# DeltaNet in the program's own order: all five engines instead of the builder's scheduler

## The chip, the core and the metric

The kernel runs on one core of one Trainium2 chip. The metric is the device time of one execution in microseconds (us). Five engines work beside each other, each through its own queue of instructions: PE (TensorE, matrix products; PEld is its loading of weights), ACT (ScalarE, functions and scaled copies), DVE (VectorE, elementwise work), POOL (GpSimd) and SP (SyncE, which here issues transfers). An instruction starts when those before it on its engine have started and what it reads and writes is free; an instruction that waits holds up everything behind it in its queue. So the order in which an engine's instructions stand matters as much as their durations.

## The reference, cut to what matters

A trunk of two layers over 256 latent tokens and 256 context tokens, 1024 wide, in fp32. Each layer is FFN, token mixer, FFN. The mixer of layer 0 is a recurrent block; the mixer of layer 1 is a gated DeltaNet in both directions, with 8 heads of 128 x 128 and chunks of 64 tokens. What it computes per head and direction, for each chunk:

```
kb    = k * beta
a_mat = strict_lower((kb @ k.T) * decay) + I
u, w  = solve(a_mat, [v * beta, kb * exp(g_cum)])     # unit lower triangular
qk    = (q @ k.T) * decay
# scan over the chunks, first the context's, then the latents'
v_new = u - w @ s
o     = q_dec @ s + qk @ v_new
s     = s * g_tot + k_dec.T @ v_new
```

q, k, v and z come from one projection `h @ w_in` (q, k, v through a convolution of four taps and SiLU; q and k are normalized). The output is `rms_norm(o) * silu(z)`, projected with `w_out` and added to the latents. Only the latents go on from there to the last FFN.

## The kernel before, in words

**Stages.** Both FFNs of layer 0, the recurrent block and the first FFN of layer 1 come first (to about 1314 us of the span), then DeltaNet (1314 to about 1626, its output projection running on from there), then the last FFN, on latents alone.

**Products.** An fp32 product is three fp32r products (L301, L302, L303: high by high, high by low, low by high). A weight tile is loaded raw, then split by an ACT cast (L165) and a DVE subtraction (L166) into a pair, in a ring of eight pairs and three raw tiles; some tiles were split earlier and are loaded as pairs by POOL's queue. `WS.step()` issues one such split.

**Projections of DeltaNet.** 32 tiles in the order eight k, eight q, then v and z mixed (`vvvvzzvzzvvzzvzz`). The first four k tiles are done together with the norm. The other 28 go through one loop: k and v tiles in two halves (context and latents), q and z in one; a half is 24 products of 256 columns. Through each half four calls of `tick(n)` are made, and these spread the other engines' work between the products:

```python
def tick(n):
    WS.step()
    if n >= PACE["decay_from"]:
        run(dec, PACE["decay_steps"])
    pipe.tick(PACE["steps"])
    if n >= PACE["keys_from"]:
        run(later, 1)
```

`pipe` holds the heads that have been projected: `conv` (ACT copy L787, three DVE operations L791), SiLU, and what q, k and v need after it (L1145, L1150; L1168 multiplies q's products into the decay). `later` is `keys()`, one of whose steps is taken per tick from tile 9 on (`keys_from` = 9). It makes the decay matrices of the eight heads (`k_rest`, L1086 to L1121, with Relu L1088 and Exp L1089 on ACT; four ticks a head), then the norms, and then

```python
for _ in solve():
    yield from pause(PACE["solve"])
```

with `PACE["solve"]` = 4. `solve` inverts the triangular blocks of all heads, chunks and directions at once: two DVE transposes, 31 elimination steps of one product (L1225, into `tm`) and one subtraction (L1228, into `Bc`), then four transposes (L1231, L1232). `merge` (L1247 to L1282) puts the 32 x 32 blocks together to 64 x 64 with small PE products. What `keys()` has not done at the end of the loop is done by `run(later)` right behind it (L1347), ahead of `pipe.drain()` and the scan.

**Scan.** 8 steps (four of the context, four of the latents) for each of 8 heads, which go in pairs. A pair passes through stages, and `advance` moves every live pair by one, the newest first. For latents: PE's p1 (L1386, state by k and q); DVE's L1394 (the right side r) and ACT's L1399 (a scaled copy of the same p1, four to a pair); PE's p2 (L1406) from r; ACT's L1409 and L1412 (two scaled copies of p2); PE's L1417 and DVE's L1424 (the new state); PE's p4 (L1430) and DVE's L1431 (added to the output).

**Readout.** `out_norm` of a head is called in `advance` when its last step is done: two squares with a sum on ACT (L1449); with the second head of a pair, a chain of small DVE operations (L1457 to L1461 and an inverse root by three Newton steps in integers and fp32, L315 to L324) and the scaling of two heads (L1463). When all pairs are through, `out_head` (PE transposes L1468, DVE L1471 and L1472, ACT cast L165, DVE L166) is called for heads 0 to 3, then for each further head ahead of the output projection's k-th batch of products. Its first residual is L750.

**What sets the order.** By default the builder's scheduler orders each engine's instructions: it simulates when each becomes ready and takes the earliest, the program's order being the priority. Where the code stands in `with eng("...")` (L151, `tc.manual_schedule`), the engines named (P: PE, A: ACT, D: DVE, G: POOL, S: SP) keep the program's order. Before, DeltaNet stands in no such block; the last FFN stands in `eng("PADGS")`.

Of the kernel before, what the change touches and what calls it, by code (L numbers as in the profile page):

```python
# [94 lines left out]
def trunk(ctx, tc, io):  # L95
# [9 lines left out]
    def nm(p):  # L105
        cnt[0] += 1
        return f"{p}{cnt[0]}"
# [4 lines left out]
    @contextmanager  # L112
    def phase(ns, nraw=0, nw=0, off=0):

        with tc.tile_pool(name=nm("ph"), bufs=1, reuse_waits="tile") as p:
            old = dict(scope)
            scope.update(s=p, ns=ns)
            if off:
                p.tile([128, off // 4], F32, name="pad1")
            if nw:  # L120
                slot("first")
            if off:
                p.tile([128, 64 - off // 4], F32, name="pad2")
            if nw:
                ring_l = Ring(p, "l", nraw, nw)
                ring_l.pair()
                ring_l.raw()
                WS.cycle("glglglglglglgg", "gggl" if nraw == 1 else "gglgl", ring_l)
            else:
                WS.cycle("g", "g", None)  # L130
            yield
            scope.clear()
            scope.update(old)
# [17 lines left out]
    def eng(E):  # L151
        return tc.manual_schedule(engines={dict(P=ET.PE, A=ET.Activation, D=ET.DVE, G=ET.Pool, S=ET.SP)[c] for c in E})
# [15 lines left out]
    class Ring:  # L168
# [8 lines left out]
        def pair(self):  # L177
            t = self.pool.tile([128, 2, 512], F32R, name=nm("wp"), tag="wp" + self.name, bufs=self.nw)
            return HL(t[:, 0], t[:, 1], t)
# [1444 lines left out]
    def front():  # L1624
        later = [t + {"q": 0, "v": 16, "z": 24}[x] for x, t in DN_ORDER[8:]]
        later = [("dn_in", t) for t in (*range(12, 16), *later)]
        outs = [("dn_out", d) for d in range(KD)]
        kept = later[PACE["kept_from"]:] + outs[:PACE["kept_out"]]
        WS.keep.extend(kept)
        norms = [Norm(0, 0), Norm(0, 1), Norm(0, 2), Norm(1, 0), Norm(1, 1, perm=True)]  # L1630
        parts = [Ffn(0, 0), Lru(), Ffn(0, 1), Ffn(1, 0)]
        WS.plan.extend((io["dn_in"][t], 1024, "g") for t in range(8, 12))
        WS.plan.append((io["dn_ab"], 256, "g"))
        assert not WS.keep
        WS.plan.extend((t, 1024, "p") if t in kept else (io[t[0]][t[1:]], 1024, "g") for t in later + outs)
        parts.append(Ffn(1, 1, (1,)))
        for i, p in enumerate(parts[:4]):
            with eng("PS" if i in (1, 2) else "PADGS"):
                if i == 0:
                    start(norms[0], p, norms[1], parts[1].prepare)  # L1640
                else:
                    p.run(norms[i], norms[i + 1], ahead=4)
        return norms[4], parts[4]

    with eng("PS"), phase(44, 2, 6):
        norm, f = front()
    adap.release()
    next_norm = Norm(1, 2, short=True)
    with tc.tile_pool(name="dns", bufs=1, reuse_waits="tile") as dns, phase(7):
        WS.ahead(4)  # L1650
        hpool = tc.alloc_tile_pool(name="hp", bufs=1, reuse_waits="tile")
        H = [hpool.tile([128, KD, 2, 256], F32R, name=nm("H"), tag=f"H{v}", bufs=1) for v in V2]
        ks = iter(range(KD))

        def pair(_):
            k = next(ks)
            return HL(*(Parts(H[0][:, k, i], H[1][:, k, i]) for i in range(2)))
        norm.pair = pair

        pools = [hpool, None, xctx]  # L1660

        def done(i):
            pools[i].release()
            if i == 2:
                pools[1] = tc.alloc_tile_pool(name="solve", bufs=1, side="right", reuse_waits="tile")

        deltanet(norm, next_norm, dns, hpool, pools, done)
    last = Norm(0, 0, short=True)
    with eng("PADGS"), phase(44, 2, 6, 192):
        WS.ahead(4)  # L1670
# [98 lines left out]
```

## Time and profile before

| | |
|---|---|
| median of 3 runs | 1841.48 us (1838.37 to 1845.29) |
| the profiled execution | 1840.58 us |
| its span | 1838.8 us |
| PE busy | 1767.9 us (96%) |
| PEld busy | 1534.4 us (83%) |
| DVE busy | 1311.3 us (71%) |
| ACT busy | 807.0 us (44%) |
| POOL busy | 105.6 us (6%) |
| chain that ended last, by engine | PE 79%, DVE 10%, ACT 5%, issue 4%, DMA 2% |

The shares are averages over stages with different limits. The stretches of DeltaNet must be looked at one by one: a table of windows gives each engine's busy time in a stretch, and a timeline of one engine gives its instructions in the order in which they ran, each with the wait before it and what ended this wait.

### The profile page before, as it was taken

To read this page: it belongs to the slowest core of one execution; us is meant where nothing else is said; L and a number is where in the kernel's file an instruction comes from. 1 tells how busy PE (TensorE), PEld (TensorE's weight loads), DVE (VectorE), ACT (ScalarE), POOL (GpSimd) and SP (SyncE) were. 2 spreads that over 40 slices of the span, in tenths; PEclk is the share of its full clock that TensorE was granted. 3 is DMA by queue.
4 is the path that set the end of the run, shared out by engine and by line. 5 is a ranking of instruction groups with operands and counts; after the bars stand their busy time and mean duration, and the time that the engine had idled before them with its cause. 6 is when DMAs were issued, how large, how long until landed. Compare 5 with 4: busy or idle time off the path is not lost.

```text
span 1838.8 us, 28624 instructions
## 1 busy us (share of the span) xinstructions
PE 1767.9 (96%) x10806; PEld 1534.4 (83%) x10806; DVE 1311.3 (71%) x2694; ACT 807.0 (44%) x1661; POOL 105.6 (6%) x146
## 2 busy tenths in 40 slices
PE   4999999999899999999999999999999989889997
PEld 3788888888778888888898888888997988689997
DVE  7877866787878767766657655555689978776565
ACT  5532222246884433233334331332478434655454
POOL 4100000000000000000000000000006330100000
PEclk9999999999999999999999999999999989989999
DMA  9354645452133666466633675654335550025653
GB/s 348 113 185 158 220 160 171 160 200 89 46 115 126 215 214 223 178 228 207 215 113 126 218 247 198 218 199 136 105 99 166 171 175 1 1 104 188 202 184 116
DMA packets 98059, 300.59 MB, mean 163 GB/s; under 512 B 10881, under 2 KB 20353, under 8 KB 97793
## 3 DMA queue, kind: packets, MB, share of 16 engines
q1 hardware_dynamic: 92160, 277.79, 44.7%
q0 software_dynamic: 5760, 20.97, 3.7%
q8 instruction: 85, 1.39, 0.3%
q14 instruction: 54, 0.43, 0.1%
HBM read 276.70 MB, written 22.02 MB: 162 GB/s over the span
## 4 chain that ended last, share of the span: by engine, by line
PE 79%; DVE 10%; ACT 5%; issue 4%; DMA 2%; POOL 0%; SPq 0%; POOLq 0%; ACTq 0%; DVEq 0%
PE gu L302 14%; PE gu L301 14%; PE gu L303 14%; PE fo L303 4%; PE fo L302 4%; PE fo L301 4%; PE tl L301 4%; PE tl L302 4%; PE tl L303 4%; DVE u L791 2%; PE p L1386 1%; PE gu L546 1%; PE gu L542 1%; PE gu L543 1%; PE p L1417 1%
## 5 line engine op out<-in xcount | busy, mean ns | idle before, releaser
L165 ACT CAST wp<-wr 128x512 fp32r<-128x512 f32 (+1 forms) x689 | 382.7, 607 | 279.8 <-DMA wr<-in_ffn_out_dram 68.1
L166 DVE TENSOR_TENSOR wp<-wr,wp 128x512 fp32r<-128x512 f32 (+1 forms) x689 | 433.5, 676 | 98.9 <-ACT wp L165 95.3
L302 PE MATMUL gu<-hl,wp 128*128 128x512 f32 (+1 forms) x1312 | 477.0, 364 | 8.0 <-DVE hl L505 8.0
L301 PE MATMUL gu<-hh,wp 128*128 128x512 f32 (+1 forms) x1312 | 476.9, 363 | 0.9 <-ACT hh L503 0.8
L303 PE MATMUL gu<-hh,wp 128*128 128x512 f32 (+1 forms) x1312 | 476.2, 363 | 0.0
L407 DVE SCALAR_TENSOR_TENSOR junk<-ar,cb 128x1024 bf16<-128x1024 f32 x224 | 273.8, 1223 | 22.6 <-DMA ar<-in_w_adaT_dram 18.8
L302 PEld LDWEIGHTS gu<-hl,wp 128*128 128x128 f32 x1312 | 247.3, 189 | 49.0 <-DVE hl L505 10.3
L301 PEld LDWEIGHTS gu<-hh,wp 128*128 128x128 f32 x1312 | 247.4, 189 | 41.2 <-ACT hh L503 1.6
L303 PEld LDWEIGHTS gu<-hh,wp 128*128 128x128 f32 x1312 | 247.5, 189 | 38.8
L657 ACT ACTIVATE sg<-gu 128x512 f32<-128x512 f32 (+1 forms) x88 | 47.9, 544 | 362.0 <-PE gu L303 352.3
L659 DVE TENSOR_TENSOR hf<-sg,gu 128x512 f32<-128x512 f32 (+1 forms) x88 | 54.5, 620 | 177.2 <-PE gu L303 130.3
L301 PE MATMUL tl<-hidh,wp 128*128 128x256 f32 (+1 forms) x418 | 139.1, 333 | 0.0
L302 PE MATMUL tl<-hidl,wp 128*128 128x256 f32 (+1 forms) x418 | 138.6, 332 | 0.0
L303 PE MATMUL tl<-hidh,wp 128*128 128x256 f32 (+1 forms) x418 | 138.6, 332 | 0.0
L301 PE MATMUL fo<-hidh,wp 128*128 128x512 f32 (+1 forms) x352 | 127.0, 361 | 0.0
L303 PE MATMUL fo<-hidh,wp 128*128 128x512 f32 (+1 forms) x352 | 127.0, 361 | 0.0
L302 PE MATMUL fo<-hidl,wp 128*128 128x512 f32 (+1 forms) x352 | 127.0, 361 | 0.0
L301 PE MATMUL f<-H,wp 128*128 128x256 f32 x320 | 93.2, 291 | 0.0
L303 PE MATMUL f<-H,wp 128*128 128x256 f32 x320 | 91.4, 286 | 1.0 <-DVE wp L166 1.0
L302 PE MATMUL f<-H,wp 128*128 128x256 f32 x320 | 91.2, 285 | 0.0
L301 PEld LDWEIGHTS tl<-hidh,wp 128*128 128x128 f32 x418 | 79.0, 189 | 7.9
L302 PEld LDWEIGHTS tl<-hidl,wp 128*128 128x128 f32 x418 | 79.0, 189 | 7.8
(322 smaller groups left out, 2794.7 us busy)
## 6 DMA issues: line engine op xcount, KB each, us to landing
wr<-in_ffn_in_dram SPq DMA_DIRECT2D x172, 512.0 KB, 4.7
ar<-in_w_adaT_dram SPq DMA_DIRECT2D x128, 512.0 KB, 3.6
wr<-in_ffn_out_dram SPq DMA_DIRECT2D x64, 512.0 KB, 4.9
kp<-wp SPq DMA_DIRECT2D x80, 256.0 KB, 7.2
wp<-kp POOLq DMA_DIRECT2D x40, 512.0 KB, 5.0
wr<-in_dn_in_dram SPq DMA_DIRECT2D x32, 512.0 KB, 3.7
wr<-in_ffn_out_dram SPq DMA_DIRECT2D x64, 192.0 KB, 3.5
wr<-in_lru_in_dram SPq DMA_DIRECT2D x16, 512.0 KB, 3.9
```

Source lines behind the costliest of these rows:

```text
L165: ACT.copy(dst.hi, src)
L166: DVE.tensor_tensor(dst.lo, src, dst.hi.bitcast(F32), OP.subtract)
L301: PE.matmul(out, w.hi, x.hi, start=start, stop=False)
L302: PE.matmul(out, w.hi, x.lo, start=False, stop=False)
L303: PE.matmul(out, w.lo, x.hi, start=False, stop=stop)
L407: DVE.scalar_tensor_tensor(junk, raw, 1.0, cb[:, v], OP.mult, OP.mult, accum_out=m[:, t % 8, v:v + 1])
L542: PE.matmul(p[:, cols], w.hi, x.hi, start=(k == 0), stop=False)
L543: PE.matmul(p[:, cols], w.lo, x.hi, start=False, stop=False)
L546: PE.matmul(p[:, cols], w(k * 128).hi, x.lo, start=False, stop=(k == KD - 1))
L657: ACT.activation(sg[:, cols], P[0][:, cols], AF.Silu)
L659: DVE.tensor_tensor(hf[:, cols], sg[:, cols], P[1][:, cols], OP.mult)
L791: DVE.scalar_tensor_tensor(uv[:, :, a:b], pv[:, :, a + sh:b + sh], cw(j), uv[:, :, a:b], OP.mult, OP.add)
```

## The change

The call of `deltanet` is put into `eng("PADGS")`: in DeltaNet each of the five engines issues its instructions in the order in which the program calls them. No instruction of the program, no size and no buffer is changed.

```diff
-        deltanet(norm, next_norm, dns, hpool, pools, done)
+        with eng("PADGS"):
+            deltanet(norm, next_norm, dns, hpool, pools, done)
```

## Rows read from the trace of the kernel before

**Rows 1.** Windows by stage: us, busy of PE, PEld, DVE, ACT, POOL, PEclk, DMA share, GB/s

```profile
1384.00:1432.00 48.00, 42.52 (x399) 36.18 (x398) 46.48 (x116) 42.97 (x86) 33.38 (x47) 0.97 0.52 162
1432.00:1445.00 13.00, 13.00 (x153) 11.87 (x153) 12.05 (x30) 6.27 (x24) 5.20 (x9) 0.85 0.25 81
1445.00:1497.00 52.00, 51.60 (x451) 51.13 (x449) 50.50 (x86) 18.70 (x52) 16.80 (x27) 1.00 0.75 231
1497.00:1521.00 24.00, 16.98 (x559) 16.29 (x560) 11.72 (x18) 9.13 (x19) 7.28 (x11) 0.72 0.26 82
...
1548.00:1601.00 53.00, 50.55 (x341) 39.83 (x340) 41.46 (x141) 35.44 (x112) 5.44 (x12) 1.00 0.00 1
1601.00:1626.00 25.00, 20.70 (x137) 19.03 (x136) 21.06 (x106) 15.16 (x56) 1.83 (x4) 0.80 0.00 1
```

**Rows 2.** Windows, line L1225 alone: us, DVE busy, PEclk, DMA share, GB/s

```profile
1474.00:1498.00 24.00, 5.72 (x12) 1.00 0.79 240
```

**Rows 3.** Windows, line L1228 alone, same columns

```profile
1474.00:1498.00 24.00, 5.75 (x12) 1.00 0.79 240
```

**Rows 4.** Timeline of DVE, end of the solve: start, us, engine, line, operation

```profile
1489.53 2.23 DVE L1231 STREAM_TRANSPOSE A<-Bc 128x1024 f32<-128x1024 f32 x1
...
1495.62 1.95 DVE L1232 STREAM_TRANSPOSE Bc<-Bc 128x1024 f32<-128x1024 f32 x1
1497.40 2.27 DVE L791 SCALAR_TENSOR_TENSOR u<-f,cst,u 128x510 f32<-128x510 f32 x3
```

**Rows 5.** Timeline of PE, the last product of the projections

```profile
1496.15 0.28 PE L303 MATMUL f<-H,wp 128*128 128x256 f32 x1
```

**Rows 6.** Timeline of DVE, readout: in brackets, idle before and its releaser

```profile
1604.62 0.16 DVE L1458 TENSOR_TENSOR rsv<-rsv,so 128x4 f32<-128x4 f32 x1 [1.26 <-ACT jk L1449]
```

**Rows 7.** The page's DMA issues: count, KB each, median us to landing

```profile
wr<-in_dn_in_dram SPq DMA_DIRECT2D x32, 512.0 KB, 3.7
```

**Rows 8.** ACT's groups by line, 1384 to 1432: count, busy us, mean ns, idle

```profile
L1150 ACT ACT_TABLE_LOAD x5 | 6.4, 1283 | 0.1
L1089 ACT ACT_TABLE_LOAD x5 | 6.4, 1283 | 0.1
```

**Rows 9.** Timeline of ACT, a table load and what follows

```profile
1384.16 1.28 ACT L1150 ACT_TABLE_LOAD   x1
1385.45 0.42 ACT L1150 ACTIVATE kq<-kq 128x256 f32<-128x256 f32 x1
```

**Rows 10.** Timeline of all engines, one cycle of the latent scan

```profile
1555.53 0.71 PE L1386 MATMUL p<-S,kq 128*128 128x128 f32 x4 [0.20 <-ACT vn L1399]
...
1557.62 0.37 ACT L1409 ACTIVATE vs<-p,bkc 128x128 f32<-128x128 f32 x1 [1.38 <-PE p L1406]
...
1558.79 1.50 ACT L1399 ACTIVATE vn<-p,egf 64x128 f32<-64x128 f32 x4
...
1559.58 0.71 PE L1386 MATMUL p<-S,kq 128*128 128x128 f32 x4 [0.28 <-ACT vn L1399]
```

**Rows 11.** Timeline of DVE, readout

```profile
1601.13 0.29 DVE L1431 TENSOR_TENSOR vn<-vn,p 128x128 f32<-128x128 f32 x1 [0.21 <-PE p L1430]
1601.51 1.46 DVE L1394 SCALAR_TENSOR_TENSOR r<-p,negc,vn 64x128 f32<-64x128 f32 x4
...
1605.21 0.17 DVE L315 TENSOR_SCALAR rsi<-rsv 128x4 int32<-128x4 int32 x1
1605.42 0.17 DVE L317 TENSOR_SCALAR ro<-rsi 128x4 int32<-128x4 int32 x1
...
1608.07 0.16 DVE L1458 TENSOR_TENSOR rsv<-rsv,so 128x4 f32<-128x4 f32 x1
...
1608.19 0.16 DVE L322 SCALAR_TENSOR_TENSOR rst<-rst,rsv 128x4 f32<-128x4 f32 x1
...
1622.21 0.42 DVE L1471 SCALAR_TENSOR_TENSOR yt<-yt,cst,z 128x192 f32<-128x192 f32 x1
...
1625.77 0.48 DVE L750 SCALAR_TENSOR_TENSOR x<-op,m,x 128x256 f32<-128x256 f32 x1
```

## The prediction, made before the changed kernel was built

> **What bounds the kernel now.** I read the page first: its chain lies mostly on PE, so the question is which engine holds each stage of DeltaNet, and what the changed order does to that engine. DeltaNet takes about 1314 to 1626 us of the span; nothing outside it is reordered. The table of windows answers it by stage [rows 1]. From 1384 to 1432 DVE is busy 46.48 of 48 us and PE 42.52: the heads' key work limits. From 1445 to 1497 PE is busy 51.60 of 52 (451 products at 0.114 us) and DVE 50.50: both are full, but PE can't be shortened and DVE holds work that could stand elsewhere. From 1497 to 1521 PE is busy 16.98 of 24 at a granted clock of 0.72, the merge, a chain: 1.2 and 2.4 GHz mixed. From 1548 to 1601 (the latent scan) PE shows 50.55 of 53 and DVE 41.46, but PE's rows there carry waits. From 1601 to 1626 (readout) no engine is full. I then read timelines of single engines where the program's order and the trace's differ.
>
> The operations and their count are the same before and after. Every effect is a wait at the head of an engine's queue, so each term is: which instruction stands first in program order, when its input comes, and what is queued behind it.
>
> **Term A, the solve.** The elimination steps (L1225, L1228) are issued by `keys()`, one call per `tick`, four ticks per half tile. From tile 9 the loop has 7 q halves, 16 v halves and 8 z halves, so 31 × 4 = 124 calls. The eight key heads take 32 of them, their drain, the norms and the first transposes some 18, so the first step comes at about call 50. With `PACE["solve"]` = 4 the calls left hold 19 of the 31 steps. The other 12, and the four transposes L1231/L1232, stand in `run(later)` behind the last projection. Before, the builder pulled these forward: the last 12 steps lie in 1474 to 1490 and the transposes at 1489.53 to 1497.57 [rows 2 to 4], while PE still projects until 1496.15 + 0.28 = 1496.43 [rows 5]; in exchange v7's conv (L791), which the program has earlier, waits until 1497.40 [rows 4].
>
> In program order DVE may not start step 19 before it has done everything that the program has ahead of it: the conv of v7, which waits for v7's products. These end two halves ahead of the loop's end, 2 × 24 × 0.114 = 5.5 us; an ACT copy, three conv operations and two steps fill most of that. So DVE reaches step 19 when the projections end. Then 12 steps cost 5.72 + 5.75 = 11.47 us [rows 2, 3], with 0.03 between operations 12.3 (estimate), and the transposes 8.04. The solve ends 20.3 us after the projections, at 1516.7 if these still end at 1496.4, against 1497.57: **+19.1**. Nothing hides it: the merge needs the transposed factors, and the scan needs the merge, 24 us in which PE now does 17.
>
> Can the projections end earlier, since DVE is relieved of 19.5 us in this stretch? At most by what PE loses now between 1384 and 1497: 5.5 + 0.4 us idle, and 48 × 0.03 + 13 × 0.15 = 3.4 us of clock [rows 1]. That puts the lower end at +19 − 9 = +10. Can they end later? In 1384 to 1432 the eight key heads run as chains DVE–ACT–POOL that the old order filled with other heads' work; if each now waits once as long as DVE waits for ACT at 1604.62 (1.26 [rows 6]), that is 8 × 1.26 = 10, so +29 at most. I take +19, since PE holds the end of the projections and the two deviations point opposite ways.
>
> The DMA issues on SP's and POOL's queues are put in program order too. The weight ring (three raw tiles, eight split pairs) covers them, so I cost them at nothing; a load that came late would cost at most its 3.7 us from issue to landing [rows 7], inside the bounds above.
>
> ACT gets something back in that stretch. The old order alternates two functions there: ten table loads in L1150 and L1089, 1.28 us each [rows 8]. In the program's order these change over about once, two loads, so eight fewer: 10.3 us less on ACT. ACT is busy 42.97 of 48, DVE 46.48, so DVE's work hides this and I put it at nothing in the sum. If DVE did wait for ACT there, the projections would come earlier, which is rival 3. The Trainium skill ("ScalarE: Activation LUTs", section "What ACT_TABLE_LOAD costs") puts a drain of about 1380 ns beside the load's 1283 ns and advises batching by table set. The trace has the 1283, but no such drain: the load starts at 1384.16 and the next activation at 1385.45, 1.29 later [rows 9]. By the page the eight loads would be an estimated 21.3 us of ACT, by the rows 10.3; the sum is the same by both as long as DVE limits there.
>
> **Term B, the latent scan.** A cycle (one p1 to the next) takes 1559.58 − 1555.53 = 4.05 us, and 53 us hold 13.4 of such cycles at the mean of 3.96. p1 (L1386) waits 0.20 and 0.28 for ACT's L1399, the four scaled copies of the pair before [rows 10]. ACT reaches these late: it first waits 1.38 for L1406's p2, does L1409 and L1412, and only then L1399 from 1558.79. The program has it the other way round: in one `advance` the newest pair's L1399 comes first and the older pair's L1409/L1412 behind. In program order L1399 can therefore start when p1 ends and run in ACT's idle 1.38, and the loop PE → ACT → PE opens. What binds next is DVE, 41.46/13.4 = 3.1 per cycle, so I take 3.2. Over 12 cycles: 12 × (3.96 − 3.2) = **−9**. Upper end 0 (a bank or the chain through r and p2 binds, nothing gained), lower end −12: the window with DVE full, 53 − 41.46.
>
> **Term C, the readout.** Four groups of two heads each have a chain of some 15 tiny DVE operations (L1457 to L1461, `rsqrt`), and then eight heads do transposes, L1471, L1472 and a split before their products. The old order weaves the groups into each other and into the heads' work. Dependent operations start 0.21 apart (1605.21, 1605.42), woven ones 0.12 or less (1608.07, 1608.19) [rows 11]. In the program all four groups come ahead of the first head, and each group's chain stands ahead of the next group's L1431, on which the next four ACT squares wait; DVE's 1.26 at 1604.62 is such a wait [rows 6]. Per group: squares 1.65 (four at about 0.41, an estimate from ACT's 0.37 for 128 columns in L1409), chain 14 starts × 0.20 = 2.8, products 0.67 (an estimate from L1431's 0.29 for 128 columns, twice and a little); four groups 20.5, plus some 2.8 for the scan's last operations (1.46 of L1394 and five L1431 at 0.29, less overlap [rows 11]), 23.3 us. Then eight heads, each L1471 at 0.42 and by that row an estimated 0.3 for L1472's third of its columns, 0.4 for an ACT cast and 0.4 for a DVE subtract, 1.5 in series: 12; then some 1.4 from the last split to the first residual. That is 36.7 from 1601.4 to the L750 at 1625.77, 24.4 before: **+12**. If the heads' chains overlap fully across DVE, ACT and PE, +4; if PE's product batches wait for each head too, +16.
>
> [...]
>
> **Term D.** Small: the inverse norm of q ahead of the first state copies (13 tiny operations at 0.20, half of them beside the merge's end: 1.3, an estimate), and PE at its lower level for somewhat longer after its longer idle (the 0.72 of 1497 to 1521 holds such a stretch): together **+2**, 0 to +4. The first stage, the context scan and the last FFN keep the order they have: ±1.
>
> **Sum.** 19 − 9 + 12 + 2 = +24. The profiled execution took 1840.6 (span 1838.8 and 1.8 around it), so 1864.6; the median of the runs is 0.9 above the profiled execution, so 1865 against 1841.5. The likeliest case's own range is 1857 to 1873.
>
> **Rivals.**
> 1. A backlog on DVE (not slower). If DVE already falls 19 us behind PE before the steps begin, the solve is DVE's queue in either order, and term A vanishes: 1841.5 + 5 = 1846. For it: DVE is busy 46.48 of 48 in 1384 to 1432. Against: from 1445 both are full in step, and PE's six rotating banks at the q tiles tie it to DVE. It decides once DVE's lag at 1445 exceeds the 19.5 us of late solve work. 0.14.
> 2. The scan isn't faster: banks of p1 to p4 bind rather than ACT's order. Then 1865 + 9 = 1874. For it: PE shows 50.55 of 53 busy. Against: the 1.38 idle of ACT. 0.15.
> 3. ACT bounds 1384 to 1432; eight loads less bring the projections forward by up to 9: 1865 − 9 = 1856. For it: ACT 42.97 of 48 with 10.3 in loads. Against: DVE's 46.48. 0.08. The Trainium skill's "Table sets: the hidden batching unit" (same page on ScalarE) is the rule that would favour it.
> 4. The key heads' chains stall in 1384 to 1432: 1865 + 10 = 1875. For it: DVE's 96% comes from woven heads. Against: `keys()` itself spreads a head over four ticks. 0.05.
> 5. The order hardly changes, because the old one followed the program where it matters: 1841. Against it stand the steps in [rows 2 to 4]. 0.02.
> 6. Rivals 1 and 3 are one: ACT's loads keep DVE behind, so without them projections and solve both come 9 earlier, A = −9: 1846 − 9 = 1837, and faster by over 0.5% once C stays under 7; at C's lower end 1829. For and against it what stands at 1 and 3. 0.04.
>
> My forecast has 0.52. A measurement of this kernel tells about 0.5% (9 us, 1832 to 1851) from no change. Faster: rival 6, 0.04. Within: rivals 1 and 5, 0.16. Slower: the rest, 0.80. The range reaches down to rival 1 and its spread, 1848, and up past rivals 2 and 4, 1882.
>
> **What would show it.** Term A: in the changed trace 12 L1225 behind the last L303 into f, the transposes behind them, and PE idle for about 20 us there. Term B: p1 to p1 of about 3.2 us, L1399 ahead of L1409. Term C: four norm chains in a row, and 36 us from the last p1 to L750. Loads: two in place of ten in 1384 to 1432. I am wrong if DVE reaches step 19 well before or after the last product, or if the scan's cycle stays at 4.

## The result, and the profile after

The changed kernel takes 1905.33 us (median of 4 runs, 1903.28 to 1911.57) against 1843.38 us before: a ratio of 1.0343, 95% interval 1.0318 to 1.0368. It is slower by 62 us where I forecast 24, above the range.

Read from the timelines of PE, DVE and ACT, DeltaNet goes like this, in us (the marks between the stages are the first product of the projection loop, its last one, the first L1406 of the scan, the first L1386 of the latents, the last row of L1417, and the first and the last L750):

| stage | before | after | change | predicted |
|---|---|---|---|---|
| projection loop | 147.6 | 178.4 | +30.8 | 0 |
| rest of the solve and merge | 24.7 | 40.7 | +16.0 | +19 |
| context scan | 25.9 | 27.9 | +2.0 | 0 to +2 |
| latent scan | 50.1 | 43.4 | −6.7 | −9 |
| end of scan and readout to L750 | 28.6 | 46.2 | +17.6 | +12 |
| output projection, first to last L750 | 14.5 | 17.5 | +3.0 | 0 |

The sum is +62.7, the difference of the two medians 62. The windows of the changed kernel (columns as in [rows 1]) are, in order, the stretch ahead of the first elimination step, the one behind the last projection, the merge, the context scan, the latent scan and the readout:

```profile
1349.00:1477.00 128.00, 101.99 (x850) 90.47 (x848) 97.40 (x216) 66.37 (x169) 39.85 (x58) 0.84 0.31 97
1527.90:1548.00 20.10, 0.32 (x4) 0.24 (x5) 19.10 (x29) 0.38 (x1) 3.90 (x5) 0.57 0.13 43
1548.00:1568.50 20.50, 17.42 (x560) 16.90 (x561) 8.06 (x11) 9.48 (x18) 5.54 (x8) 0.67 0.17 54
1568.50:1596.50 28.00, 26.45 (x271) 20.66 (x268) 23.50 (x93) 9.53 (x30) 0.00 (x0) 1.00 0.01 2
1596.50:1640.00 43.50, 39.20 (x319) 32.61 (x320) 39.10 (x133) 32.19 (x103) 4.54 (x10) 1.00 0.01 1
1640.00:1686.00 46.00, 24.27 (x161) 22.25 (x161) 29.77 (x120) 18.20 (x64) 2.72 (x6) 0.70 0.00 1
```

The same window of the kernel before, up to its own first elimination step:

```profile
1349.00:1445.00 96.00, 89.85 (x837) 81.22 (x836) 89.76 (x209) 76.05 (x177) 42.45 (x58) 0.95 0.41 130
```

The first step (L1225) comes at 1476.81 in place of 1445.52, 31 us later. DVE idled 6 us on the way to it before (96 − 89.76) and 31 after (128 − 97.40); the rest is 8 us of work that the old order put behind it. From the first step to the end of the last projection it is 51 us in both kernels (to 1496.43 and 1527.87), so the whole loss of the loop lies ahead of the first step.

**Behind the last projection** the picture is the one forecast. PE's timeline of the changed kernel, and DVE's, its middle left out:

```profile
1527.59 0.28 PE L303 MATMUL f<-H,wp 128*128 128x256 f32 x1
1542.75 0.32 PE L1247 MATMUL pp<-A,MO 32*32 32x32 f32 x4 [14.89 <-DVE A L1231]
```

```profile
1528.26 0.66 DVE L1225 TENSOR_TENSOR tm<-N,Bc 128x480 f32<-128x480 f32 x1
...
1540.34 0.22 DVE L1228 TENSOR_TENSOR Bc<-Bc,tm 128x62 f32<-128x62 f32 x1
1540.60 2.00 DVE L1231 STREAM_TRANSPOSE A<-Bc 128x1024 f32<-128x1024 f32 x1
...
1546.00 1.85 DVE L1232 STREAM_TRANSPOSE Bc<-Bc 128x1024 f32<-128x1024 f32 x1
```

From 1527.87 to 1547.85 there are 20.0 us (20.3 were forecast), where before the transposes ended 1.1 us behind the last product [rows 4, 5].

**Ahead of it** is what I missed. DVE's waits in the projection loop, 1349 to 1477 of the changed kernel (engine, what it would write, releaser: us in total, times, longest):

```profile
DVE wp L166 <- ACT wp L165: 13.6, 9, 2.0
DVE u L791 <- ACT u L787: 11.0, 5, 3.9
DVE gc L1029 <- PE gc L1027: 3.2, 1, 3.2
```

and ACT's in the same stretch:

```profile
ACT e L1088 <- DVE e L1086: 16.3, 7, 2.4
ACT kq L1145 <- DVE u L791: 15.6, 8, 2.3
ACT kq L1067 <- DVE u L791: 10.0, 3, 4.9
```

ACT and DVE wait for each other, 77 us in all in this stretch (the waits of ACT for DVE and of DVE for ACT added up) against 10 before. For PE they waited 10 us against 14, so PE's products, slower at a granted clock of 0.84 in place of 0.95 (102 us busy for 850, 90 for 837), are not what holds them up; nor did ACT wait for a load. One key head shows the exchange; DVE first, then ACT, both from the timeline of the changed kernel:

```profile
1418.04 0.69 DVE L166 TENSOR_TENSOR wp<-wr,wp 128x512 fp32r<-128x512 f32 x1 [1.90 <-ACT wp L165]
1418.64 0.99 DVE L791 SCALAR_TENSOR_TENSOR u<-f,cst,u 128x255 f32<-128x255 f32 x2
...
1422.83 0.68 DVE L1086 TENSOR_TENSOR e<-gr,gc 128x512 f32<-128x512 f32 x1
...
1426.63 0.69 DVE L166 TENSOR_TENSOR wp<-wr,wp 128x512 fp32r<-128x512 f32 x1 [1.91 <-ACT wp L165]
```

```profile
1420.80 0.41 ACT L1145 COPY kq<-u 128x256 f32<-128x256 f32 x1 [1.91 <-DVE u L791]
1423.55 0.63 ACT L1088 ACTIVATE e<-e 128x512 f32<-128x512 f32 x1 [2.35 <-DVE e L1086]
1424.21 0.63 ACT L1089 ACTIVATE e<-e 128x512 f32<-128x512 f32 x1
1424.75 1.20 ACT L1121 COPY MO<-e 32x128 f32<-32x128 f32 x4
1425.98 0.62 ACT L165 CAST wp<-wr 128x512 fp32r<-128x512 f32 x1
```

DVE works 5.5 us (1418.04 to 1423.51), ACT takes over for 2.4, then casts the next weight (0.65), for which DVE has waited 1.9. The cast itself needs nothing from DVE; it stands behind four instructions that do. A head takes 8.6 us this way. From the first to the last of the eight L1086 it is 7.8 us a head on the mean in the changed kernel and 5.4 in the kernel before.

**The scan and the readout.** One cycle of the latent scan after, and the four norm groups on DVE, with the first L1471 and the first L750 behind them:

```profile
1612.35 1.46 DVE L1394 SCALAR_TENSOR_TENSOR r<-p,negc,vn 64x128 f32<-64x128 f32 x4 [0.16 <-PE p L1386]
1613.15 1.50 ACT L1399 ACTIVATE vn<-p,egf 64x128 f32<-64x128 f32 x4 [0.67 <-DVE r L1394]
1614.68 0.37 ACT L1409 ACTIVATE vs<-p,bkc 128x128 f32<-128x128 f32 x1
...
1615.68 1.46 DVE L1394 SCALAR_TENSOR_TENSOR r<-p,negc,vn 64x128 f32<-64x128 f32 x4 [0.16 <-PE p L1386]
```

```profile
1647.06 0.16 DVE L1458 TENSOR_TENSOR rsv<-rsv,so 128x4 f32<-128x4 f32 x1 [2.49 <-ACT jk L1449]
...
1649.84 0.76 DVE L1463 TENSOR_TENSOR vn<-vn,ro 128x256 f32<-128x256 f32 x2
1650.61 1.46 DVE L1394 SCALAR_TENSOR_TENSOR r<-p,negc,vn 64x128 f32<-64x128 f32 x4
...
1655.21 0.16 DVE L1458 TENSOR_TENSOR rsv<-rsv,so 128x4 f32<-128x4 f32 x1 [2.49 <-ACT jk L1449]
...
1661.06 0.16 DVE L1458 TENSOR_TENSOR rsv<-rsv,so 128x4 f32<-128x4 f32 x1 [1.84 <-ACT jk L1449]
...
1666.63 0.16 DVE L1458 TENSOR_TENSOR rsv<-rsv,so 128x4 f32<-128x4 f32 x1 [1.56 <-ACT jk L1449]
...
1670.08 0.41 DVE L1471 SCALAR_TENSOR_TENSOR yt<-yt,cst,z 128x192 f32<-128x192 f32 x1
...
1686.09 0.88 DVE L750 SCALAR_TENSOR_TENSOR x<-op,m,x 128x256 f32<-128x256 f32 x2 [0.35 <-PE op L303]
```

PE's last p1 of the changed kernel:

```profile
1644.07 1.16 PE L1386 MATMUL p<-S,kq 128*128 128x128 f32 x8 [0.32 <-ACT oq L1399]
```

L1399 now stands ahead of L1409, and the cycle is 3.33 us (1612.35 to 1615.68) against 3.96 on the mean before. In the readout, a chain takes 2.78 us (1647.06 to 1649.84) as forecast, but the groups lie 8.15, 5.85 and 5.57 apart, where I had 5.12: the last pair's L1394 stands behind the first group's chain (1650.61), and DVE waits up to 2.49 for the squares.

### The profile page after: what moved, and what is told of

Read it like the earlier page. It is cut to its first block, busy times and chain, and to the rows that moved or that the text cites. A ratio compares the mean times of both kernels' runs of the same rounds, so it can differ in the third digit from the quotient of the medians.

```text
span 1909.5 us, 28633 instructions
## 1 busy us (share of the span) xinstructions
PE 1779.7 (93%) x10806; PEld 1546.0 (81%) x10806; DVE 1323.6 (69%) x2694; ACT 794.9 (42%) x1651; POOL 102.8 (5%) x146
## 4 chain that ended last, share of the span: by engine, by line
PE 77%; DVE 11%; ACT 6%; issue 4%; DMA 2%; SPq 0%; POOL 0%; POOLq 0%; ACTq 0%; DVEq 0%
PE gu L302 14%; PE gu L301 14%; PE gu L303 14%; PE fo L302 4%; PE fo L301 4%; PE fo L303 4%; PE tl L301 3%; PE tl L303 3%; PE tl L302 3%; DVE u L791 2%; DVE wp L166 1%; PE p L1417 1%; PE gu L546 1%; PE gu L542 1%; PE gu L543 1%
## 5 line engine op out<-in xcount | busy, mean ns | idle before, releaser
L303 PE MATMUL gu<-hh,wp 128*128 128x512 f32 (+1 forms) x1312 | 478.0, 364 | 0.0
L303 PEld LDWEIGHTS gu<-hh,wp 128*128 128x128 f32 x1312 | 249.0, 190 | 39.0
L303 PE MATMUL tl<-hidh,wp 128*128 128x256 f32 (+1 forms) x418 | 139.1, 333 | 0.0
L303 PE MATMUL fo<-hidh,wp 128*128 128x512 f32 (+1 forms) x352 | 127.4, 362 | 0.0
L301 PE MATMUL f<-H,wp 128*128 128x256 f32 x320 | 95.0, 297 | 3.6 <-ACT wp L165 3.6
L303 PE MATMUL f<-H,wp 128*128 128x256 f32 x320 | 92.6, 289 | 1.1 <-DVE wp L166 1.1
L302 PE MATMUL f<-H,wp 128*128 128x256 f32 x320 | 92.2, 288 | 0.0
L303 PEld LDWEIGHTS tl<-hidh,wp 128*128 128x128 f32 x418 | 79.3, 190 | 7.8
```

Of the source, the lines that this page charges most:

```text
L301: PE.matmul(out, w.hi, x.hi, start=start, stop=False)
L302: PE.matmul(out, w.hi, x.lo, start=False, stop=False)
L303: PE.matmul(out, w.lo, x.hi, start=False, stop=stop)
```

## The experiments

Stages are the rows of the table above: loop, solve and merge, context scan, latent scan, readout to L750. Edits are shown against the changed kernel unless it says "before". Each kernel has one trace. The two kernels at the end of this section, which leave everything ahead of the scan to the scheduler, have in the loop the same instructions in the same order as the kernel before, on PE, DVE, ACT and POOL, and their loops take 145.4 where its own took 147.6. So 2 us between the loops of two traces show nothing.

**The yield** tested the first theory: ACT and DVE hand the work to and fro, and one step apart would open the loop.

```diff
+            yield
             ACT.activation(e, e, AF.Relu, scale=-1.0)
```

> The changed kernel with one yield more in each key head, between DVE's subtraction (L1086) and ACT's Relu and Exp (L1088, L1089), so that these two stand behind the next tick's weight cast on ACT's queue. Theory H (hand-over): in program order ACT and DVE pass the work to and fro once per key head, 5.5 us on DVE, 2.4 on ACT and 0.65 for the cast, 8.6 in all, and each waits while the other works; the yield opens this loop. H expects a key head's period of at most 7 us in place of 8.6, the last projection 10 to 16 us earlier than the 1527.9 of the changed kernel, and a total of 1889 to 1895. Rival P: PE's own order (products that wait for a bank at the head of PE's queue, and the lower clock behind them) sets the pace, ACT's and DVE's waits only follow. P expects the period to stay at 8.6 and the total at 1905 within 4.

1904.11 us (2 runs); loop 171.2. A head's period fell to between 5.4 and 6.3 from the fourth head on, as H said, and stayed at 8.0 to 8.8 ahead of it. After the twentieth half the loop was 20 us ahead of the changed kernel's; at its end 7.2 were left. Half of the difference went in the next half, where PE waited 6.2 us for ACT at the products of q. DeltaNet as a whole is 6.0 shorter in the trace and the profiled execution 5.6 (1905.98 for 1911.57), while the medians, of two and of four runs, differ by 1. This is below H's size, and against P's "no change" in the loop.

**One engine freed, one engine bound.**

```diff
-        with eng("PADGS"):
+        with eng("PDGS"):    # and "P", "A", "D"
```

> The changed kernel, but ACT alone is left to the builder's scheduler in DeltaNet (PE, DVE, POOL and SP in program order). H: ACT may take a weight cast while it would wait for DVE, so at least half of the 31 us lost ahead of the last projection comes back (last projection by 1512), while the 12 late elimination steps on DVE stay behind it (solve 19 us behind the last projection, as in the changed kernel); in the scan ACT's old order may return and cost up to 7. Total 1885 to 1897. P: the last projection stays at 1527.9 within 4, total 1903 or more.

1906.78 us; loop 170.9, latent scan 47.1, readout 45.8. Freeing ACT gave 7.5 us of 31 in the loop, less than H asked for, more than P allowed, and took back 3.7 in the latent scan. Neither holds as written.

> PE alone in program order in DeltaNet, the other four engines left to the builder's scheduler. H (ACT and DVE hold each other up in order, PE follows): the last projection ends within 6 us of the 1496.4 of the kernel before, the total is 1840 to 1852. P (PE's own order sets the 31 us): the last projection ends at 1515 or later, the total is 1860 or more.

1842.45 us (8 runs), ratio 0.9995, interval 0.9967 to 1.0022; loop 151.4, latent scan 46.7. PE's order costs nothing in the total, and 3.8 us of 31 in the loop: rival P is out.

> ACT alone in program order in DeltaNet. H in its first form (a loop that needs both queues in order) expects less than 8 us lost ahead of the last projection, total up to 1852; nine table loads fewer than in the kernel before. Rival A (ACT's order is what holds the others up): 15 us or more there, total above 1856.

1863.72 us; loop 168.6 (+21.0), solve and merge 24.4, latent scan 43.7, readout 28.9. Rival A holds in the loop. DVE's waits ahead of the first step:

```profile
DVE u L791 <- ACT u L787: 5.7, 2, 4.1
DVE wp L166 <- ACT wp L165: 4.6, 5, 2.0
DVE gc L1029 <- PE gc L1027: 3.3, 1, 3.3
DVE qk L1105 <- ACT e L1089: 2.6, 3, 2.1
```

> DVE alone in program order in DeltaNet. With ACT free, PE, DVE, POOL and SP in order still lost 23 us ahead of the last projection, and PE's order alone cost nothing. If DVE's own order holds the stage (rival D: a full engine that waits at its head has nothing to put in the gap), this kernel loses 17 to 25 us ahead of the last projection and 19 more in the late solve, and in the readout some 10: total 1880 to 1895. H in its first form (both queues needed) expects less than 10 us ahead of the last projection, and with solve and readout 1862 to 1875.

1904.62 us: as much as the changed kernel loses, though made up otherwise. Loop 164.4 (+16.8), solve and merge 41.9, context scan 32.9, latent scan 50.5, readout 45.4. Rival D has the loop and the solve about right; the total lies above its range, with 7 us more in the context scan, which nobody forecast, and 17 in the readout in place of 10. H in its first form, a loop that needs both queues in order, falls; either queue alone is enough. POOL's and SP's order was tried only together with others. In this kernel DVE's waits ahead of the first step are for others:

```profile
DVE u L791 <- ACT u L787: 8.8, 7, 3.9
DVE qk L1105 <- ACT e L1089: 2.7, 3, 1.8
```

**The two halves of DeltaNet.** Program order only up to the end of the merge, and only from there on (before, with the block opened or closed behind `done(1)`):

> Program order on all five engines only up to the end of the merge; the scan and the readout are left to the builder's scheduler. If the parts add up as the two traces read (31 us ahead of the last projection, 19 for the late solve, 3 regained in the merge, and 14 from the scan to the output projection), this kernel takes 1843 + 47 = 1890. A rival in which the scan's and the readout's loss comes from what the late front leaves behind (lower clock, late weights) expects 1900 to 1905.

1897.26 us (1892.71 and 1901.81); loop 178.5, solve and merge 41.7, context scan 29.9, latent scan 50.4, readout 28.4. The two runs lie on both sides of what tells the hypotheses apart, but the stages settle it: latent scan and readout are as before (50.1 and 28.6), so the rival falls. The traced execution, 1892.71, is 52 above that of the kernel before; 4 of these are a longer context scan, which no run explains.

> The other half: the builder's scheduler up to the end of the merge, program order from the scan on. By addition 1843 + 11 to 14 = 1854 to 1857, with the latent scan's cycle below 3.6 us and the readout some 17 us longer. The rival (the loss is left behind by the front) expects 1843 within 4.

1855.68 us; loop 145.5, latent scan 43.4, readout 46.1. As expected: the scan's gain and the readout's loss don't come from the front.

**The late steps.**

```diff
-    ... "key_steps": 3, "solve": 4, ...
+    ... "key_steps": 3, "solve": 2, ...
```

> The changed kernel with an elimination step at every second call of the key work in place of every fourth, so that all 31 steps and the transposes are issued ahead of the last projection. If term A is what the prediction says (12 steps and four transposes behind the projections, 19 to 20 us), the solve ends within 4 us of the last projection. DVE was busy some 35 of 50 us between 1480 and 1530; with 20 more it is full, so the last projection comes 3 to 8 us later. Output projection (first L750) 11 to 17 us earlier than 1686, total 1888 to 1896. The rival, that the merge waits for something else, expects no more than 4 us gained.

1893.16 us. The solve ends at 1535.24, 12.9 us ahead of the last projection (1548.13), and solve's rest and merge behind the projections fall from 40.7 to 9.6; but the loop grows from 178.4 to 195.6: 6.4 us up to its last two halves, 10.8 in these, where the merge's products now stand in PE's queue among the projections. 14 us are gained between the loop's start and the scan, about as expected, but by another way: counted from the loop's start the last projection came 17 later, not 3 to 8.

**PE's wait at the q tiles.**

```diff
-    ... "q_lag": 2, ...
+    ... "q_lag": 8, ...
```

> The changed kernel with six pauses more in each q head between ACT's SiLU and square (L1150, L1053) and PE's products of q (L1159), so that projections stand between them in PE's queue. If PE's 8.3 us wait at L1159 for L1150 is a loss by PE's order, 4 to 8 us come back: last projection at 1520 to 1524, total 1897 to 1902. If DVE, which is behind at that point, sets the pace, the wait only changes its place: last projection at 1527 within 2, total 1905 within 3.

1902.93 us; loop 175.7, 2.7 better, hardly more than two traces differ by. After the twentieth half the kernel was 12 us ahead of the changed one, three halves later 7, six halves later 3: most of the wait changed its place.

**The decays.**

```diff
-    "decay_from": 6, ...
+    "decay_from": 4, ...
```

> The changed kernel with the chain of the decays started two tiles earlier (tile 4 in place of tile 6), one step per tick as before. Ahead of the ninth half PE lost 9 us in the changed kernel, at products (L1027) that stand behind this chain. If that is a loss of its own, 4 to 8 us come back at the tenth half and stay: last projection at 1520 to 1524, total 1897 to 1901. If DVE's queue only shifts it into the key heads, the last projection stays within 2 us of 1527.9 and the total within 3 of 1904.

1906.46 us; loop 180.3. No gain: the loss moved from the ninth half to the fifth, and the sum came out the same within 2 us.

**The readout's groups.**

```diff
-    "readout": "1 3 5 7", ...
+    "readout": "3 7", ...
```

> The changed kernel with two norm groups of four heads in the readout in place of four groups of two: two chains of some 15 tiny DVE operations fewer, and none between the first pairs' last scan stages. If the chains in program order are what costs the readout its 12 us and more, L750 comes 6 to 9 us earlier (1677 to 1680), total 1896 to 1899. If the heads' own work (transposes, L1471, L1472, split) sets the readout, it stays at 1686 within 2.

1898.51 us; readout 38.2 in place of 46.2, loop 178.4. Two chains fewer, with their waits for squares, gave 8.0 of the 17.6 us, as forecast. That the two chains left cost as much again was not tried.

**Everything on which ACT waited, moved down.** The yield, and pauses ahead of L1145 and L1067:

```diff
+                yield from pause(2)
                 ACT.copy(kv, uv)
...
-            yield from pause(2)
+            yield from pause(4)
             state["k", hd] = True
```

> The changed kernel with everything in which ACT stood waiting for DVE at the head of its queue moved down by one or two ticks: Relu and Exp of a key head (L1088, L1089; ACT waited 16 us there), the copy of a q head (L1145; 16 us) and the SiLU of a k head (L1067; 10 us). H2: DVE bounds the stage, and what it waits for are weight casts (L165, 13.6 us) and conv copies (L787, 11.0 us) that stand behind ACT's waiting instructions. H2 expects these two waits to halve at least, the last projection at 1514 or earlier in place of 1527.9, total at most 1893. Rival D: DVE's own order costs 17 us there whatever ACT does, so no more comes back than the 7 of the single yield: last projection at 1518 to 1521, total 1897 or more.

1893.90 us; loop 167.9, last projection at 1518.40. DVE's two waits fell from 24.6 to 18.1, by a quarter and not by half:

```profile
DVE wp L166 <- ACT wp L165: 9.7, 10, 2.2
DVE u L791 <- ACT u L787: 8.4, 4, 3.9
```

ACT's waits in the same stretch (L1089 and L1147 are here the L1088 and L1145 of the changed kernel):

```profile
ACT e L1089 <- DVE e L1086: 17.6, 6, 3.9
ACT kq L1067 <- DVE u L791: 10.0, 3, 4.9
ACT kq L1147 <- DVE u L791: 2.7, 4, 1.2
```

10.5 us of 31 came back, 20 stayed, near the 17 that DVE's order costs alone. Rival D's floor fits better than H2, though the total is between both. But only the wait at the copy of q went (15.6 to 2.7); those at Relu and at k's SiLU stayed, so ACT still stood where H2 wanted it gone, and H2 is not refuted by this run.

**Three mends at once** (yield, `solve` 2, two groups):

> The changed kernel with three mends at once: the yield in each key head (7 us by its own run), an elimination step at every second call (some 11), two norm groups in the readout (6). If they add up, 24 us come back: total 1878 to 1884, still slower than before by some 38. If they share one limit (DVE's queue ahead of the last projection), only 15 to 18: 1886 to 1891.

1878.19 us: they add up, and program order stays 2% behind (1.0194, 1.0164 to 1.0224).

**The one part that was faster, by itself.** Before, with the block only around the latent steps, closed ahead of the first norm group:

```diff
             s, hd = divmod(n, 8)
+            if n == 32:
+                es = ExitStack()
+                es.enter_context(eng("PADGS"))
+            if n == 60:
+                es.close()
```

> The kernel before, with program order on all five engines only in the latent scan, from its first pair of the first latent step to just before the first norm group of the readout. If term B holds by itself (the cycle from p1 to p1 falls from 3.96 to about 3.4 us), the last L1417 comes 5 to 7 us earlier than before relative to the first p1, and with the scheduler left to the readout the gain stays: total 1833 to 1838. The rival: the gain needs the whole scan and readout in order, or the readout's order under the scheduler worsens, total 1841 or more.

1835.02 us (7 runs) against 1842.30 for the kernel before: ratio 0.9956, interval 0.9939 to 0.9972. Latent scan 43.4, readout 28.8. This version is faster than both kernels, by 0.4% against the kernel before.

> The kernel before with ACT alone in program order, and only in the latent scan (the same stretch as in the run with all five engines there). If term B is ACT's order (L1399 of the newest pair ahead of L1409 and L1412 of the older one), the scan's gain of 6 to 7 us is the same as with five engines and the total 1833 to 1838. The rival: with PE and DVE left to the scheduler the gain halves, total 1838 to 1841.

1837.10 us (12 runs) against 1841.45, ratio 0.9969, interval 0.9952 to 0.9986; latent scan 43.4 again. ACT's order is enough to shorten the scan by the whole 6.7. PE's order alone had shortened it by 3.4, DVE's alone not at all (50.5).

## Why the prediction was wrong

**The step that failed** is the one on the projections' end: "I take +19, since PE holds the end of the projections and the two deviations point opposite ways", with a bound of ten us for the key heads' waits. The projection loop became 30.8 us longer. Without that the other stages come to +31.9, inside the range. I had read DVE's 46.48 of 48 us [rows 1] as what hides ACT's gain, and not drawn the other conclusion: an engine that busy has little room to wait, and here its idle time went from 6 us to 31. My bound took one wait per head, 1.26 us from the readout [rows 6]. What came are nine waits for weight casts (13.6 us) and five for conv copies (11.0) ahead of the first step. In the key heads the cast stands behind ACT instructions that wait for DVE, 1.9 us a head; the longest wait for a conv copy, 3.9 at the start of the loop, stands behind an ACT copy that waits for PE (L1003). Rival 4 named the stall with a price of ten; it was the right mechanism with a third of its size, and not in the key heads alone. Half by half against the kernel before, 9.8 us were lost ahead of the first key head, most of them with the decays' products (L1027), 16.7 in the eight halves of the key heads and 7.5 at the first products of q (L1159); 3 came back behind them. By the single engines, ACT's order costs 21 us in the loop, DVE's 17, PE's 4.

**Term A's own part was right**: 12 steps and four transposes behind the projections, 20.0 us measured for 20.3; it is DVE's order (41.9 for solve and merge with DVE alone in order, 24.4 with ACT alone). The merge then went 2.9 us faster (20.7 for 23.6), which I had not priced and no run explains.

**ACT's table loads** came about as forecast, nine fewer for eight: in the whole loop L1089 keeps one, L1150 none. ACT's row of the changed kernel, 1396 to 1470, against the two of [rows 8]:

```profile
L1089 ACT ACT_TABLE_LOAD x1 | 1.3, 1283 | 0.0
```

No gain from them can be seen, and ACT, busy 66.37 of 128 us, had time for the old ones; but no run has the loads changed by themselves. The Trainium skill ("ScalarE: Activation LUTs", section "Table sets: the hidden batching unit") advises the batching; rival 3, which it favoured, fell.

**Term B** had the right mechanism and the sign: 3.33 us a cycle for 3.2, −6.7 for −9; it is ACT's order (43.4 with ACT alone). Rival 2 fell.

**Term C** was mis-sized: +17.6 for +12. As the working counted, from the last p1 (its end, 1645.23) to L750, it takes 40.9 us for the 36.7 forecast, and 23.9 before by the same reading. Of this the groups up to the first L1471 take 24.9 for 23.3, the heads and their products 16.0 for 13.4. The chain was right (2.78 for 2.8); the distance of the groups was not, 6.5 on the mean of three for 5.12. The groups' squares cost DVE 2.49 to 1.56 of waiting, and the first group's chain holds up the last pair's scan step. It is DVE's order: readout 45.4 with DVE alone, 28.9 with ACT alone. In this chain dependent operations start 0.20 apart where woven ones started 0.12 apart or less [rows 11].

**Term D** had +2 and measured +2.0 in the context scan, but no run shows its two parts. The output projection's +3.0 was priced at nothing, and what makes it was not tried.

**Rival 1**, the backlog, fell: the 20.0 us of late solve came behind the projections, and DVE was not behind by its work, it waited. What stays open is why ACT's 21 and DVE's 17 make 31 together and not 38: the runs show that the two don't add up, not which waits they share.

## What to carry to other kernels

Program order on an engine that is nearly full can cost what that engine then waits, though the others have time free: here DVE's idle time rose by 24 us where the loop grew by 31. Ask of each instruction in its queue whether what it reads stands behind a wait on the other engine. A stage whose waits form a ring (here p1, L1399, p1) can gain from program order, so bind the order by stage and by engine: in this kernel ACT alone, in the latent scan alone, is worth 4 us by the medians and 6.7 by its stage, and the rest is better left to the scheduler. Work that a generator hands out per tick must be counted against its ticks, or its tail lands behind the loop.

## What the runs showed of the hardware

The last FFN ran at two paces, at a granted clock of 1.00 in both. PE's L303 in the kernel before, then in the changed one:

```profile
1749.79 0.28 PE L303 MATMUL gu<-hh,wp 128*128 128x256 f32 x1
1750.13 0.28 PE L303 MATMUL gu<-hh,wp 128*128 128x256 f32 x1
```

```profile
1749.97 0.28 PE L303 MATMUL gu<-hh,wp 128*128 128x256 f32 x1
1750.33 0.28 PE L303 MATMUL gu<-hh,wp 128*128 128x256 f32 x1
```

A product takes 0.1133 us in the one and 0.1178 in the other, from the first FFN product behind DeltaNet to the last; from there to the end of the kernel this is some 7 us. In the output projection just ahead it is the other way round: 0.1178 before, 0.1133 in the changed kernel, so the pace can change within one execution. In the last FFN the traces with the yield, with ACT freed, with PE alone in order and with all five engines in order in the latent scan show 0.1178, all the others 0.1133, with the whole of DeltaNet in order in both groups; so it doesn't follow the order of DeltaNet. It lies in the changed kernel's profiled execution (1911.57) and is why I compare stages, not spans. What sets it was not tried.
